# A down projection of eight units in three passes over the channels, 512 columns wide, with stores that add

## The chip, the core and the metric

The kernel runs on one NeuronCore of a Trainium2 chip. Its engines have a queue of instructions each: TensorE (PE in the profile) multiplies matrices, VectorE (DVE) and ScalarE (ACT) work on rows, GpSimd (POOL) does the same and issues some transfers, and SyncE (SP) issues most of them. Engines wait for each other and for transfers by semaphores. The metric is the device time of one execution in microseconds (us).

## What is computed

One layer of a decoder trunk on 2048 rows of 1024 channels: a mixer (sliding-window attention and a gated recurrence), then a gated MLP with a short causal convolution, then a norm. The part that matters here is the end:

```python
h = rms_norm(x, ffn_norm_g[l]) * (1 + scale_f) + shift_f
u, v = jnp.split(h @ w_up[l], 2, axis=-1)                # w_up: 1024 x 2 * 2816
u = causal_depthwise_conv(u, conv_w[l], conv_b[l])
x = x + gate_f * ((jax.nn.silu(u) * v) @ w_down[l])      # w_down: 2816 x 1024
...
return rms_norm(x, final_norm_g)
```

All of it is float32. x as it stands before the MLP is called x1; it lies in DRAM as 16 tiles of 128 rows, `x1_d` (the trace calls them x_d).

## The kernel before

**Products.** Both projections of the MLP multiply 2 x 2 blocks with seven products instead of eight (Strassen's scheme in Winograd's form), and each float32 product is made of three matmuls: both operands are split into a high part that the matmul takes exactly and the low rest, and `mm3` issues high x high, high x low, low x high. An operand is therefore seven blocks (four of the matrix, and sums of them), once as h and once as l: `Th`, `Tl` for the activations, `Sh`, `Sl` for the weights. ACT writes the h part, DVE (in places POOL) subtracts to get the l part.

**Up stage.** For each of 22 blocks of 128 channels and each half of the rows (`up`, banks `ps_u`) PE makes seven products of 512 columns; DVE and ACT make the convolution, silu and the gate into `cc`. Two blocks make a pair, j = 0 to 10; `combine_a` on POOL forms the sums of the pair's blocks (`sm` and in place) and POOL's queue stores the seven blocks to `act_d` in DRAM. `combine_w` prepares the weights' sums (`wc_d`) during the second half.

**Down stage.** It goes by `DSTEPS`: 2 halves of the 1024 output columns (dh), 8 units of 256 rows (tp), 11 pairs (j). A step has 7 products x 3 = 21 matmuls of 128x256 into seven banks (`ps_d`), which sum over the 11 pairs. For each half the S operands of all 11 pairs are resident. `build_s` loads a pair's raw blocks (`Sr`, from w_down and from `wc_d`) and splits them; half 0's are built at its first eight steps, half 1's at the steps that the table `SWITCH` gives, from the fifth pair of half 0's last unit on into the first unit of half 1. The tiles of S lie where tiles of the up stage lay, so a pair's build waits for the last reader of that memory; `S_PLACE` sets which. The activations of a step are loaded (`da`, four buffers) and split (`Th`, `Tl`, three buffers each) by `ahead`, some steps before they are used.

**A unit's end** (`d_unit` behind its loop). ACT and DVE sum the seven banks into `o` (256 rows of 512 columns), DVE multiplies by the gate (`dgate`) and adds x1's columns (`dx`), ACT squares. Half 0 stores the result times `dfin` (the norm's gain) to `xf_d`; half 1 loads that back (`df`), forms the root from both halves' squares, scales, and stores both halves to the output.

**What sets the order.** A scheduler orders each engine's instructions; `pin(True, SY)` keeps SP's in the order of the program, for the first eight steps of the stage and a few more loads.

Of the kernel before, what the change touches and what calls it, by code (L numbers as in the profile page):

```python
# [18 lines left out]
P = 128  # L19
# [34 lines left out]
def kernel(ctx, tc, x, c, ada_w, ada_b, mix_norm_g, w_in, b_in, attn_sinks, attn_out_g,  # L54
# [26 lines left out]
    wc_d = [[dram.tile([P, 4, 256], F32, name=f"wc_d{i}_{j}") for j in range(NJ)] for i in range(2)]  # L81
    xf_d = [dram.tile([P, 2, 512], F32, name=f"xf_d{i}") for i in range(NB // 2)]
# [1223 lines left out]
    for hf_ in range(T // HT):  # L1306
        for ff in range(NFF):
            cur = ups
            if ff + 1 < NFF:
                ups = prep_up(hf_, ff + 1)  # L1310
            elif hf_ == 0:
                ups = prep_up(1, 0)
            combine_acts(hf_, ff - 1)
            up(hf_, ff, cur, orders.get((hf_, ff), order))
            if hf_ == 0 and ff == 0:
                turn_block(*pend)
            if hf_ == 0 and ff in (4, 8, 12, 16):
                combine_t(ff // 4 - 1)
            if hf_ == 1 and ff < NFF - 2:
                for i in range(2 if ff > 17 else 1):  # L1320
                    combine_w(*divmod(ff if ff < 18 else 2 * ff + i - 18, NJ))
        combine_acts(hf_, NFF - 1)
# [7 lines left out]
    dr = ctx.enter_context(tc.tile_pool(name="dr", bufs=1, reuse_waits="tile"))  # L1330
    do = ctx.enter_context(tc.tile_pool(name="do", bufs=1, reuse_waits="tile"))


    S_LATE = ("8h", "8l", "9h", "9l", "10h", "10l")
    S_PLACE = ("2h", "0h", "3h", "0l", "T", "1h", "1l", "2l", "3l", "4l", "5l", "6l", "7l", "6h", "7h", "4h", "5h")

    def place(key):
        return ctx.enter_context(tc.tile_pool(name=f"ds{key}", bufs=1, reuse_waits="tile"))
    places = {key: place(key) for key in S_LATE}
    places["u"] = place("u")  # L1340
    for key in S_PLACE:
        places[key] = place(key)
    dt_ = places["T"]
    dss = ctx.enter_context(tc.tile_pool(name="dss", bufs=1, reuse_waits="tile"))

    sops = {}

    def s_op(j, hl, name, dt):
        return places[f"{j}{hl}"].tile([P, 7, 256], dt, tag=f"S{j}{hl}", name=name)

    def load_s(dh, j):

        nm = f"{dh}_{j}"
        c0 = dh * 512
        if j + 2 < NJ:
            r = s_op(j + 2, "h", f"Sr{nm}", F32)
            SY.dma_start(out=r[:, 0, :], in_=wdn_v[2 * j * P:(2 * j + 1) * P, c0:c0 + 256])
            SY.dma_start(out=r[:, 1:3, :], in_=wdn_v[(2 * j + 1) * P:(2 * j + 2) * P, c0:c0 + 512]
                         .rearrange("p (c n) -> p c n", c=2))
            SY.dma_start(out=r[:, 3:7, :], in_=wc_d[dh][j])  # L1360
            return [(slice(0, 7), r)]
        parts = []
        for i, src in enumerate((wdn_v[2 * j * P:(2 * j + 1) * P, c0:c0 + 256],
                                 wdn_v[(2 * j + 1) * P:(2 * j + 2) * P, c0:c0 + 512],
                                 wc_d[dh][j][:, 0:2, :], wc_d[dh][j][:, 2:4, :])):
            n = 1 if i == 0 else 2
            r = dr.tile([P, 2, 256], F32, tag="raw", bufs=4, name=f"dw{nm}_{i}")[:, 0:n, :]
            SY.dma_start(out=r, in_=src.rearrange("p (c n) -> p c n", c=n) if i < 2 else src)
            parts.append((slice(max(2 * i - 1, 0), 2 * i + 1), r))
        return parts  # L1370

    def build_s(dh, j):
        parts = load_s(dh, j)
        hi, lo = (s_op(j, hl, f"S{dh}_{j}{hl}", F32R) for hl in "hl")
        for sl, r in parts:
            n = sl.stop - (2 if dh == 0 and NJ - 2 > j >= 4 else 2 if dh and j + 2 < NJ else 0)
            S.activation(hi[:, sl, :], r, AF.Copy)
            V.tensor_tensor(out=lo[:, sl.start:n, :], in0=r[:, 0:n - sl.start, :], in1=hi[:, sl.start:n, :].bitcast(F32),
                            op=ALU.subtract)
            if n < sl.stop:  # L1380
                G.tensor_tensor(out=lo[:, n:, :], in0=r[:, n:, :], in1=hi[:, n:, :].bitcast(F32), op=ALU.subtract)
        sops[dh, j] = hi, lo

    raws, tts, seen = {}, {}, set()
    DSTEPS = [(dh, tp, j) for dh in range(2) for tp in range(NB // 2) for j in range(NJ)]

    def load_a(step):
        dh, tp, j = step
        nm = f"{dh}_{tp}_{j}"
        r = dr.tile([P, 7, P], F32, tag="raw", bufs=4, name=f"da{nm}")  # L1390
# [14 lines left out]
    ssall = const.tile([P, NB // 2, 2], F32, name="ssall")  # L1405

    def d_bank(name):
        turn[0] += 1
        return bank(name, ring8[turn[0] % 8])[:, 0:256]
# [10 lines left out]
    def d_unit(dh, tp):  # L1420
        nm = f"{dh}_{tp}"
        ps = {p: d_bank(f"ps_d{nm}_{p}") for p in DORDER}
        o = do.tile([P, 2, 512], F32, tag="o", name=f"o{nm}")
        u = places["u"].tile([P, 256], F32, tag="u", bufs=2, name=f"u{nm}")
        c11, c12, c21, c22 = o[:, 0, 0:256], o[:, 0, 256:], o[:, 1, 0:256], o[:, 1, 256:]

        def add(dst, p, other):
            V.tensor_tensor(out=dst, in0=ps[p], in1=other, op=ALU.add)

        sums = {1: lambda: S.activation(u, ps[1], AF.Copy), 2: lambda: add(c11, 2, u), 6: lambda: add(u, 6, u),  # L1430
                7: lambda: add(c21, 7, u), 5: lambda: (add(c22, 5, c21), add(u, 5, u)), 4: lambda: add(c21, 4, c21),
                3: lambda: add(c12, 3, u)}
        for j in range(NJ):
            ahead((dh, tp, j), 3 - (j == NJ - 1))
            th, tl = tts.pop((dh, tp, j))
            sh, sl = sops[dh, j]
            for p in DORDER:
                a, b = DPROD[p]
                mm3(ps[p], th[:, a, :], tl[:, a, :], sh[:, b, :], sl[:, b, :], j == 0, j == NJ - 1)
                if j == NJ - 1:  # L1440
# [85 lines left out]
```

## Time and profile before

| | |
|---|---|
| median of 3 runs | 2494.3 us (2492.16 to 2494.49) |
| profiled execution | 2490.66 us, its span 2488.9 us |
| PE busy | 2323.8 us, 93% of the span |
| DVE busy | 1911.0 us, 77% |
| ACT busy | 1055.6 us, 42% |
| POOL busy | 919.4 us, 37% |
| DMA | 389.90 MB, 157 GB/s over the span |
| last up matmul, last down matmul | 1972.0 and 2475.7 us from the span's start |

The span runs from the first to the last event of the profiled execution; its own time is a little longer. Shares are means over stages that differ, so what the down stage is limited by is read from that stretch of time. Matmuls' ends are modelled; the distance of their starts is the measure of their pace.

### The profile page before, as it was taken

To read this page: it belongs to the slowest core of one execution; us is meant where nothing else is said; L and a number is where in the kernel's file an instruction comes from. 1 tells how busy PE (TensorE), PEld (TensorE's weight loads), DVE (VectorE), ACT (ScalarE), POOL (GpSimd) and SP (SyncE) were. 2 spreads that over 40 slices of the span, in tenths; PEclk is the share of its full clock that TensorE was granted. 3 is DMA by queue.
4 is the path that set the end of the run, shared out by engine and by line. 5 is a ranking of instruction groups with operands and counts; after the bars stand their busy time and mean duration, and the time that the engine had idled before them with its cause. 6 is when DMAs were issued, how large, how long until landed. Compare 5 with 4: busy or idle time off the path is not lost.

```text
span 2488.9 us, 35680 instructions
## 1 busy us (share of the span) xinstructions
PE 2323.8 (93%) x13369; PEld 2010.0 (81%) x13369; DVE 1911.0 (77%) x2743; ACT 1055.6 (42%) x1776; POOL 919.4 (37%) x743
## 2 busy tenths in 40 slices
PE   5889898998989899999999999999999789997997
PEld 4778786887878688887888887788888679997997
DVE  8888778888876876568888888788877776676665
ACT  3336434623733454454333334333332344455443
POOL 6222212222322221225757564788888410011000
PEclk8999999999999999999999999999999889998999
DMA  7343233323322247664444245455454577687776
GB/s 213 90 119 98 81 91 96 94 69 101 95 68 85 85 159 246 204 204 131 139 129 144 93 140 189 158 159 163 161 157 166 199 260 218 211 283 263 260 243 203
DMA packets 337304, 389.90 MB, mean 157 GB/s; under 512 B 14069, under 2 KB 258763, under 8 KB 337131
## 3 DMA queue, kind: packets, MB, share of 16 engines
q1 hardware_dynamic: 326571, 347.25, 44.8%
q0 software_dynamic: 10560, 40.37, 4.4%
q8 instruction: 105, 1.72, 0.3%
q14 instruction: 68, 0.56, 0.1%
HBM read 293.71 MB, written 93.86 MB: 156 GB/s over the span
## 4 chain that ended last, share of the span: by engine, by line
PE 66%; DVE 13%; DMA 7%; POOL 6%; issue 5%; ACT 2%; SPq 0%; DVEq 0%; ACTq 0%; POOLq 0%
PE ps_u L46 24%; PE ps_d L46 15%; PE ps_o L46 5%; PE lv L46 3%; PE ps_hg L46 3%; PE ps_hq L46 2%; PE ps_hf L46 2%; PE ps_i L46 2%; PE att_o L46 2%; DVE ada L46 2%; DMA ada<-in_ada_w_dram 1%; POOL s L46 1%; PE ps_q L46 1%; DVE raw L46 1%; POOL sm L46 1%
## 5 line engine op out<-in xcount | busy, mean ns | idle before, releaser
L46 DVE TENSOR_TENSOR Tl<-da,Th 128x896 fp32r<-128x896 f32 x176 | 201.5, 1154 | 119.9 <-ACT Th L46 119.8
L46 ACT ACTIVATE Th<-da 128x896 fp32r<-128x896 f32 x176 | 166.5, 949 | 194.6 <-PE ps_d L46 161.5
L46 DVE SCALAR_TENSOR_TENSOR cc<-ub,cols,cc 128x1024 f32<-128x1024 f32 x88 | 153.4, 1743 | 14.3 <-ACT cc L46 12.0
L46 PE MATMUL lv<-a_q,K 128*128 128x128 f32 (+2 forms) x768 | 78.6, 262 | 43.8 <-DVE K L46 39.7
L46 PEld LDWEIGHTS lv<-a_q,K 128*128 128x128 f32 (+2 forms) x768 | 70.4, 173 | 56.5 <-DVE K L46 28.2
L46 DVE TENSOR_TENSOR cc<-cc,v 128x1024 f32<-128x1024 f32 x44 | 64.9, 1476 | 44.5 <-ACT cc L46 44.5
L46 POOL TENSOR_TENSOR s<-wu_0r,s 128x512 f32<-128x512 f32 x44 | 59.3, 1347 | 107.4 <-DVE ws_0l L46 14.8
L46 ACT ACTIVATE cc<-cc 128x1024 f32<-128x1024 f32 x44 | 46.7, 1060 | 122.5 <-DVE cc L46 122.5
L46 POOL TENSOR_TENSOR s<-wu_1r 128x512 f32<-128x512 f32 x44 | 68.8, 1563 | 70.1 <-DVE t_T4l L46 15.8
L46 POOL TENSOR_TENSOR wu_1r<-wu_0r,wu_1r 128x512 f32<-128x512 f32 x44 | 92.9, 2111 | 3.1
L46 POOL MEMSET AT<- 128x512 f32 x16 | 8.5, 532 | 230.3 <-PE ho L46 208.3
L46 POOL TENSOR_TENSOR pl<-raw,ph 128x512 fp32r<-128x512 f32 x32 | 44.6, 1395 | 101.2 <-ACT ph L46 101.2
L46 POOL TENSOR_SCALAR rv_d<-ssd 128x2 f32<-128x2 f32 x8 | 1.5, 192 | 208.5 <-DVE ssd L46 208.5
L46 POOL TENSOR_TENSOR S_0l<-Sr,S_0h 128x512 fp32r<-128x512 f32 x1 | 2.6, 2601 | 201.9 <-ACT S_0h L46 201.9
L46 POOL TENSOR_TENSOR s<-s,wu_0r 128x512 f32<-128x512 f32 x44 | 73.7, 1674 | 0.0
L46 DVE TENSOR_TENSOR v<-ps_u,v 128x512 f32<-128x512 f32 x88 | 60.4, 686 | 15.5 <-PE ps_u L46 12.2
L46 DVE COPY_PREDICATED AT<-lev,lv 128x512 f32<-128x512 uint32 (+1 forms) x96 | 70.0, 729 | 2.4 <-PE lv L46 1.1
L46 DVE TENSOR_TENSOR ada<-ada,cond 128x1024 f32<-128x1024 f32 (+1 forms) x37 | 54.9, 1483 | 15.3 <-DMA ada<-in_ada_w_dram 13.9
L46 ACT ACTIVATE cc<-ub,cols 128x1024 f32<-128x1024 f32 x44 | 54.5, 1240 | 24.7 <-DVE ub L46 24.7
L46 DVE TENSOR_TENSOR a_q<-a_q,tot 128x256 f32<-128x256 f32 x96 | 52.8, 550 | 9.5 <-PE lv L46 8.5
L46 DVE TENSOR_TENSOR ub<-ps_u,u 128x512 f32<-128x512 f32 x88 | 60.0, 682 | 0.1
L46 DVE TENSOR_TENSOR ot<-ps_o,gate 128x512 f32<-128x512 f32 x32 | 22.0, 688 | 46.6 <-PE ps_o L46 45.6
(2138 smaller groups left out, 9178.8 us busy)
## 6 DMA issues: line engine op xcount, KB each, us to landing
da<-act_d SPq DMA_DIRECT2D x176, 448.0 KB, 4.0
wu_0r<-in_w_up_dram SPq DMA_DIRECT2D x44, 512.0 KB, 4.5
wu_1r<-in_w_up_dram SPq DMA_DIRECT2D x44, 512.0 KB
act_d<-cc POOLq DMA_DIRECT2D x44, 512.0 KB, 4.0
ada<-in_ada_w_dram SPq DMA_DIRECT2D x40, 512.0 KB, 6.4
act_d<-sm POOLq DMA_DIRECT2D x22, 768.0 KB, 4.2
x<-in_x_dram SPq DMA_DIRECT2D x26, 512.0 KB, 5.8
Sr<-wc_d SPq DMA_DIRECT2D x18, 512.0 KB, 7.1
```

The lines of the kernel that those rows point to most:

```text
L46: ins = fn(*args, **kwargs)
```

## The change

The stage's order is turned over. Instead of two halves of the columns with all 11 pairs resident, there are three passes over the pairs (0 to 2, 3 to 5, 6 to 10), each over all 8 units and all 1024 columns: `DSTEPS` has 88 steps of 21 matmuls of 128x512. A pass sums only over its own pairs. At a unit's end passes 0 and 1 multiply by the gate and hand both tiles of 128 rows to POOL's queue, whose transfer adds them to `x1_d` (`accum_op=ALU.add`); pass 2 loads the so summed `x1_d`, adds its own part, and makes the norm and the output. `xf_d`, `dx` of half 0 and `df` go.

Five places for a pair's S operands take turns (pair j uses place j modulo 5). The first three pairs are loaded raw into places that are free until later (`load_first`) and split in four parts; every later pair is brought in two half loads through two buffers (`half_rows`, which are also used for x1 in pass 2), each split in place of use when `bring` says. SP is in the order of the program for the whole stage. `combine_w` forms the same weight sums from other loads. The last pair's activations of the second half of rows are stored raw (`raw_d`) by POOL's queue, and `last_pair` loads, combines and stores them behind step (0, 1, 0).

The diff, cut to its core:

```diff
-    wc_d = [[dram.tile([P, 4, 256], F32, name=f"wc_d{i}_{j}") for j in range(NJ)] for i in range(2)]
-    xf_d = [dram.tile([P, 2, 512], F32, name=f"xf_d{i}") for i in range(NB // 2)]
+    wc_d = [dram.tile([P, 4, 512], F32, name=f"wc_d{j}") for j in range(NJ)]
+    raw_d = dram.tile([P, 2, HT], F32, name="raw_d")
...
-        combine_acts(hf_, NFF - 1)
+        if hf_ == 0:
+            combine_acts(hf_, NFF - 1)
+        else:
+            for i in range(2):
+                G.dma_start(out=raw_d[:, i, :], in_=acts[i])
...
+    PASSES = (range(0, 3), range(3, 6), range(6, NJ))
+    NS = 5
...
+    def half_rows(name):
+        return places["part"].tile([P, D], F32, tag="sp", bufs=2, name=name)
+    S_PARTS = (slice(0, 1), slice(1, 3), slice(3, 5), slice(5, 7))
...
+    def new_s(j):
+        sops[j] = [s_op(f"{j % NS}{hl}", f"S{j}{hl}", F32R) for hl in "hl"]
+    def load_first(j):
+        r = s_op(("3h", "3l", "4h")[j], f"Sr{j}", F32)
+        for i, sl in enumerate(S_PARTS):
+            load_part(j, i, r[:, sl, :])
+            chunks[j, i] = r[:, sl, :]
+    def load_chunks(j, ii):
+        for i in ii:
+            sl = S_PARTS[i]
+            n = sl.stop - sl.start
+            chunks[j, i] = half_rows(f"Sp{j}_{i}").rearrange("p (a n) -> p a n", a=2)[:, 0:n, :]
+            load_part(j, i, chunks[j, i])
+    def split_chunks(j, ii):
+        if j not in sops:
+            new_s(j)
+        hi, lo = sops[j]
+        for i in ii:
+            sl = S_PARTS[i]
+            split(chunks.pop((j, i)), hi[:, sl, :], lo[:, sl, :], lo_eng=V)
...
-    DSTEPS = [(dh, tp, j) for dh in range(2) for tp in range(NB // 2) for j in range(NJ)]
+    DSTEPS = [(pi, tp, j) for pi in range(3) for tp in range(NB // 2) for j in PASSES[pi]]
...
-        return bank(name, ring8[turn[0] % 8])[:, 0:256]
+        return bank(name, ring8[turn[0] % 8])
...
+        if pi < 2:
+            for i in (1, 0):
+                V.tensor_tensor(out=o[i], in0=o[i], in1=dgate, op=ALU.mult)
+                G.dma_start(out=x1_d[2 * tp + i], in_=o[i], accum_op=ALU.add)
             return
...
+        for i in (1, 0):
+            V.tensor_tensor(out=o[i], in0=o[i], in1=dgate, op=ALU.mult)
+            V.tensor_tensor(out=o[i], in0=o[i], in1=prev[i], op=ALU.add)
+            S.activation(prev[i], o[i], AF.Square, accum_out=ss[:, i:i + 1])
+        r = rstd_of(places["ss"], ss, 2, D, f"d{tp}")
+        for i in (1, 0):
+            V.scalar_tensor_tensor(out=o[i], in0=o[i], scalar=r[:, i:i + 1], in1=dfin, op0=ALU.mult, op1=ALU.mult)
+            parts.append((out_v[(2 * tp + i) * P:(2 * tp + i + 1) * P, :], o[i]))
...
+    behind(0, 1, 0, last_pair)
+    def bring(j, steps):
+        behind(*steps[0], load_chunks, j, (0, 1))
+        behind(*steps[1], split_chunks, j, (0, 1))
+        behind(*steps[1], load_chunks, j, (2, 3))
+        behind(*steps[2], split_chunks, j, (2, 3))
+    bring(3, ((0, 3, 0), (0, 3, 1), (0, 3, 2)))
+    bring(4, ((0, 5, 0), (0, 5, 1), (0, 5, 2)))
+    bring(5, ((0, 6, 2), (0, 7, 0), (0, 7, 1)))
+    bring(6, ((1, 2, 3), (1, 2, 4), (1, 2, 5)))
+    bring(7, ((1, 4, 3), (1, 4, 4), (1, 4, 5)))
+    bring(8, ((1, 6, 5), (1, 7, 3), (1, 7, 4)))
+    bring(9, ((1, 7, 4), (1, 7, 5), (2, 0, 6)))
+    bring(10, ((2, 0, 6), (2, 0, 7), (2, 0, 8)))
```

Three places show how the engines' rows move. The first is ACT's queue at the start of the down stage (cc_21 is the last gated block, its second row there is silu; S0h is pair 0's high part, Th that of step 0). Before:

```order
L46 ACTIVATE cc_21_16833<-ub_21_16730,cols 128x1024
L46 ACTIVATE cc_21_16833<-cc_21_16833 128x1024
L46 ACTIVATE S_0h<-Sr_0_16936 128x1792
L46 ACTIVATE Th_0_0_16946<-da_0_0_16944 128x896
L46 ACTIVATE S_1h<-Sr_1_16950 128x1792
L46 ACTIVATE Th_0_1_16960<-da_0_1_16958 128x896
```

and now:

```order
L46 ACTIVATE cc_21_16837<-ub_21_16734,cols 128x1024
L46 ACTIVATE S0h<-Sr_16906 128x512
L46 ACTIVATE S0h<-Sr_16906 128x1024
L46 ACTIVATE cc_21_16837<-cc_21_16837 128x1024
L46 ACTIVATE S0h<-Sr_16906 128x1024 x2
L46 ACTIVATE Th_0_16937<-da_0_16911 128x896
L46 ACTIVATE S1h<-Sr_16913 128x512
L46 ACTIVATE S1h<-Sr_16913 128x1024 x3
L46 ACTIVATE Th_1_16951<-da_1_16918 128x896
```

S0h is now made in four pieces, two of them ahead of silu, and Th stands behind the fourth. The second place is PE's first step of the stage (ps_d_0_1 is product 1's bank of unit 0). Before:

```order
L46 MATMUL ps_d_0_1_16988<-S_0h,Th_0_0_16946 128x256
L46 MATMUL ps_d_0_2_16989<-S_0h,Th_0_0_16946 128x256
L46 MATMUL ps_d_0_6_16990<-S_0h,Th_0_0_16946 128x256
L46 MATMUL ps_d_0_7_16991<-S_0h,Th_0_0_16946 128x256
L46 MATMUL ps_d_0_5_16992<-S_0h,Th_0_0_16946 128x256
L46 MATMUL ps_d_0_1_16988<-S_0l,Th_0_0_16946 128x256
```

and now:

```order
L46 MATMUL ps_d_0_1_16969<-S0h,Th_0_16937 128x512
L46 MATMUL ps_d_0_1_16969<-S0l,Th_0_16937 128x512
L46 MATMUL ps_d_0_1_16969<-S0h,Tl_0_16938 128x512
L46 MATMUL ps_d_0_2_16970<-S0h,Th_0_16937 128x512
L46 MATMUL ps_d_0_2_16970<-S0l,Th_0_16937 128x512
L46 MATMUL ps_d_0_2_16970<-S0h,Tl_0_16938 128x512
```

Before, five products had their high matmuls ahead of the first that needs a low part; now the second and the third matmul need S0l and Tl. The third place is SP's queue at the last change of weights (Sr and Sp are raw weights, da raw activations, wc_d_119 to wc_d_121 the sums of pairs 8 to 10). Before, in the first unit of half 1:

```order
L46 DMA da_0_4_19711<-act_d_4_93 128x896
L46 DMA Sr_5_19734<-in_w_down_dram 128x256
L46 DMA Sr_5_19734<-in_w_down_dram 128x512
L46 DMA Sr_5_19734<-wc_d_5_127 128x1024
L46 DMA da_0_5_19747<-act_d_5_94 128x896
L46 DMA xf_d_140<-o_7_19337 128x1024
L46 DMA da_0_6_19774<-act_d_6_95 128x896
```

and now, from the last unit of pass 1 into the first of pass 2:

```order
L46 DMA Sp_2_18664<-wc_d_119 128x1024
L46 DMA Sp_3_18666<-wc_d_119 128x1024
L46 DMA da_8_18672<-act_d_8_97 128x896
L46 DMA Sp_0_18699<-in_w_down_dram 128x512
L46 DMA Sp_1_18701<-in_w_down_dram 128x1024
L46 DMA da_9_18739<-act_d_9_98 128x896
L46 DMA Sp_2_18747<-wc_d_120 128x1024
L46 DMA Sp_3_18749<-wc_d_120 128x1024
L46 DMA da_10_18766<-act_d_10_99 128x896
L46 DMA Sp_0_18793<-in_w_down_dram 128x512
L46 DMA Sp_1_18795<-in_w_down_dram 128x1024
L46 DMA da_6_18801<-act_d_6_95 128x896
```

A pair was three loads into a tile of its own; now it is four, two at a time, each into one of the two buffers behind the loads that used it last.

## Rows read from the trace of the kernel before

**Rows 1.** The page's slices: busy tenths of PE in 40 equal slices.
```profile
PE   5889898998989899999999999999999789997997
```

**Rows 2.** Windows, down stage, ps_d alone: us, busy us (count) per engine, clock, DMA.
```profile
1972.00:2060.00 88.00, 66.87 (x458) 63.28 (x459) 2.68 (x7) 0.75 (x2) 0.86 0.83 284
2060.00:2200.00 140.00, 140.00 (x1159) 139.06 (x1158) 13.61 (x36) 1.83 (x5) 1.00 0.72 220
2200.00:2300.00 100.00, 86.24 (x644) 82.86 (x643) 7.94 (x21) 0.75 (x2) 0.93 0.80 276
2300.00:2475.70 175.70, 175.00 (x1441) 173.14 (x1439) 17.47 (x46) 2.58 (x7) 1.00 0.76 247
```

**Rows 3.** The same view over 100 us of the up stage, ps_u alone.
```profile
1840.00:1940.00 100.00, 100.00 (x439) 82.01 (x438) 22.84 (x34) 2.59 (x5) 1.00 0.49 158
```

**Rows 4.** Timeline of PE, down stage's start: start, duration, operation, idle before, releaser.
```profile
1971.62 0.39 PE L46 MATMUL ps_u<-t_T4h,wvs_21l 128*128 128x512 f32 x1
1977.50 1.43 PE L46 MATMUL ps_d<-S_0h,Th 128*128 128x256 f32 x5 [5.49 <-ACT Th L46]
...
1985.87 1.68 PE L46 MATMUL ps_d<-S_1l,Th 128*128 128x256 f32 x7
1987.36 1.03 PE L46 MATMUL ps_d<-S_1h,Tl 128*128 128x256 f32 x7
...
1996.75 1.86 PE L46 MATMUL ps_d<-S_2l,Th 128*128 128x256 f32 x7 [7.53 <-DVE S_2l L46]
```

**Rows 5.** Timeline of ACT, same stretch.
```profile
1973.96 1.06 ACT L46 ACTIVATE cc<-cc 128x1024 f32<-128x1024 f32 x1 [5.41 <-DVE cc L46]
...
1976.51 0.93 ACT L46 ACTIVATE Th<-da 128x896 fp32r<-128x896 f32 x1
```

**Rows 6.** Timeline of DVE, same stretch.
```profile
1976.64 2.87 DVE L46 TENSOR_TENSOR S_0l<-Sr,S_0h 128x1792 fp32r<-128x1792 f32 x1 [0.36 <-DMA Sr<-in_w_down_dram]
...
1994.67 2.03 DVE L46 TENSOR_TENSOR S_2l<-Sr,S_2h 128x1792 fp32r<-128x1792 f32 x1 [7.96 <-issue]
```

**Rows 7.** Tile act_d, 1960 to 2000 us: who waited for it, landing.
```profile
  DVE S_2l L46: 8.0, 1
...
DMA to landing us min/median/max: 7.8/8.3/8.9
```

**Rows 8.** Groups of DVE's instructions by form, whole span.
```profile
L46 DVE TENSOR_TENSOR Tl<-da,Th 128x896 fp32r<-128x896 f32 x176 | 201.5, 1154 | 119.9 <-ACT Th L46 119.8
...
L46 DVE TENSOR_TENSOR v<-ps_u,v 128x512 f32<-128x512 f32 x88 | 60.4, 686 | 15.5 <-PE ps_u L46 12.2
...
L46 DVE TENSOR_TENSOR o<-o,dgate 128x1024 f32<-128x1024 f32 x16 | 19.5, 1218 | 0.0
```

**Rows 9.** Timeline of PE after a wait, up stage; six rows between.
```profile
1956.99 0.79 PE L46 MATMUL ps_u<-t_T2h,ws_21l 128*128 128x512 f32 x1 [3.33 <-DVE ws_21l L46]
...
1960.12 0.40 PE L46 MATMUL ps_u<-t_T2h,ws_21h 128*128 128x512 f32 x1
```

**Rows 10.** Window at the down stage's start, all engines.
```profile
1972.00:1980.00 8.00, 1.88 (x8) 1.58 (x8) 6.47 (x5) 6.04 (x6) 3.65 (x3) 0.82 1.02 387
```

**Rows 11.** Timeline of ACT at the second half's weights.
```profile
2252.28 1.70 ACT L46 ACTIVATE S_6h<-Sr 128x1792 fp32r<-128x1792 f32 x1 [2.88 <-DMA Sr<-wc_d]
```

**Rows 12.** DMA issues, 1960 to 2489 us: count, KB each, median to landing.
```profile
da<-act_d SPq DMA_DIRECT2D x176, 448.0 KB, 4.0
Sr<-wc_d SPq DMA_DIRECT2D x18, 512.0 KB, 7.1
...
xf_d<-o SPq DMA_DIRECT2D x8, 512.0 KB, 4.3
```

**Rows 13.** Timeline at the program's end: PE, DVE, ACT.
```profile
2475.46 0.28 PE L46 MATMUL ps_d<-S_10h,Tl 128*128 128x256 f32 x1
...
2476.63 0.41 DVE L46 TENSOR_TENSOR o<-ps_d,u 128x256 f32<-128x256 f32 x1
...
2484.20 1.33 ACT L46 ACTIVATE df<-df,rr_d 128x512 f32<-128x512 f32 x2 [3.27 <-DMA df<-xf_d]
```

More of the change, by code (lines that the diff above doesn't have):

```diff
@@ L1339 @@
[L1339 to L1382, printed above, removed]
+        return ctx.enter_context(tc.tile_pool(name=f"d_{key}", bufs=1, reuse_waits="tile"))
@@ new lines, with s_op @@
+    places = {key: place(key) for key in ("raw", "u", "o", "2l", "2h", "1l", "1h", "3h", "0h", "0l", "T", "4l", "gate",
+                                          "part", "3l", "4h", "fin", "ss")}
+    sops, chunks = {}, {}
+    def s_op(key, name, dt):
+        return places[key].tile([P, 7, 512], dt, tag=f"S{key}", name=name)
+    def half_rows(name):
+        return places["part"].tile([P, D], F32, tag="sp", bufs=2, name=name)
+    S_PARTS = (slice(0, 1), slice(1, 3), slice(3, 5), slice(5, 7))
@@ L1422, in d_unit, with stores @@
+    parts = []
+    def stores():
+        while parts:
+            dst, src = parts.pop(0)
+            SY.dma_start(out=dst, in_=src)
+    def d_unit(pi, tp):
+        js = PASSES[pi]
+        nm = f"{pi}_{tp}"
         ps = {p: d_bank(f"ps_d{nm}_{p}") for p in DORDER}
-        o = do.tile([P, 2, 512], F32, tag="o", name=f"o{nm}")
-        u = places["u"].tile([P, 256], F32, tag="u", bufs=2, name=f"u{nm}")
-        c11, c12, c21, c22 = o[:, 0, 0:256], o[:, 0, 256:], o[:, 1, 0:256], o[:, 1, 256:]
+        prev = o = u = None
@@ L1427, in add @@
         def add(dst, p, other):
             V.tensor_tensor(out=dst, in0=ps[p], in1=other, op=ALU.add)
[L1430 to L1436, printed above, removed]
+        for j in js:
+            ahead((pi, tp, j), 3 - (j == js[-1]))
+            if j == js[1]:
+                stores()
+            if j == js[-2] and pi == 2:
+                prev = [half_rows(f"dx{tp}_{i}") for i in range(2)]
+                for i in range(2):
+                    SY.dma_start(out=prev[i], in_=x1_d[2 * tp + i])
+            th, tl = tts.pop((pi, tp, j))
+            sh, sl = sops[j]
+            if j == js[-1]:
+                o = [places["o"].tile([P, D], F32, tag="o", bufs=3, name=f"o{nm}_{i}") for i in range(2)]
+                u = places["u"].tile([P, 512], F32, tag="u", name=f"u{nm}")
+                c11, c12, c21, c22 = o[0][:, 0:512], o[0][:, 512:], o[1][:, 0:512], o[1][:, 512:]
+                sums = {1: lambda: S.activation(u, ps[1], AF.Copy), 2: lambda: add(c11, 2, u), 6: lambda: add(u, 6, u),
+                        7: lambda: add(c21, 7, u), 5: lambda: (add(c22, 5, c21), add(u, 5, u)),
+                        4: lambda: add(c21, 4, c21), 3: lambda: add(c12, 3, u)}
@@ L1500 @@
+    stores()
+    pin(False, SY)
 _INS = ['x', 'c', 'ada_w', 'ada_b', 'mix_norm_g', 'w_in', 'b_in', 'attn_sinks', 'attn_out_g', 'hgrn_lb_logits',
```

144 lines of the change are left out of this document (63 added, 81 removed).

## The prediction, made before the changed kernel had run

> **What bounds the kernel now.** The slices of the profile's page come first [rows 1]: in the last fifth of the span, the last nine slices of 62 us, PE is busy 9 tenths or more in five; 7 and 8 where the stage begins, 7 in the slice from 2240 us, 7 at the end. PE is the bound there, with holes. The windows over the stage size them [rows 2]. Between 2060 and 2200 us nothing holds PE: 1159 matmuls of 256 columns in 140.00 us, 0.1208 us each, at a granted clock of 1.00. The stage issues 2 halves x 8 units x 11 pairs x 21 = 3696 of them, 446.5 us at that pace, and lasts from the last up matmul (1972.0) to the last down matmul (2475.7), 503.7 us. So 57.2 us are lost, nearly all in two windows: 88.00 us with 458 matmuls (55.3 us of work), 32.7 lost at the stage's start; 100.00 us with 644 (77.8), 22.2 lost where the second half's weights come; and 1.6 in the last window. The window of the up stage, where matmuls are 512 wide, gives 439 in 100 us at clock 1.00, 0.2278 us each [rows 3].
>
> The sum is made against the profiled run's 2490.7 us (span 2488.9 and 1.8 around it); the median of the runs shown, 2494.3, lies 3.6 above it, and those 3.6 are put back at the end.
>
> **Pace: -25.5.** The change issues (3 + 3 + 5) x 8 x 21 = 1848 matmuls of 512 columns for the same work. At 0.2278 us that is 421.0 instead of 446.5. The two paces differ by 0.2278 - 2 x 0.1208 = -0.0138 us for equal columns, so a matmul costs here about 14 ns beyond its columns at either width, and half the matmuls save that half. A rule speaks against this: the Trainium skill, "TensorE: Matmul & The Clock Gate", section Back-to-back issue gap, gives a warm matmul its columns at 2.4 GHz plus some 2.5 ns. An estimate by that page is 109 ns and 216 ns for the two widths, and a gain of 4.7 us only; the trace does not agree with its size, and the row's pace is what the sum uses.
>
> **Start: -21.7.** Now PE waits twice [rows 4]: 5.49 us for ACT's first Th, and 7.53 us for DVE's S_2l, and from 1977.50 it runs at half pace to 1987.36 at least (seven matmuls of 256 in 1.49 us from the row at 1985.87 to that one). Ahead of the first Th ACT does the gated activation's silu at 1973.96 and then S_0h [rows 5]; both stay in the changed order, with two small parts of S0h ahead of silu. From silu's 1973.96, 1.0 for it, two parts of 1.0 and Th's 0.93 put the first matmul at 1977.9, 0.4 later than now. The wait for S_2l goes: DVE's S_2l began 7.96 us late [rows 6], and it is the one that waited 8.0 us for the stores of POOL's combined acts, which took 8.3 us to land [rows 7]: the memory of S_2l had been that of the combined tile. The change takes that combination out of the path: the last pair is stored raw and combined later. What is late next is the third matmul (S0h with Tl), because products are now finished one by one: DVE has behind the last gating 0.69 + 3 x 1.22 for S0l in its four parts (durations by [rows 8]: 686 ns for 512 columns, 1218 ns for 1024), then Tl 1.15, and a multiplication of the gate: Tl_0 is there at about 1980.6. Pairs 1 and 2 follow at 0.69 + 3 x 1.22 + 1.15 = 5.5 us each, so Tl_2 at 1991.6, and its step of 4.8 us ends at 1996 to 1998. Without any wait three steps of 21 x 0.2278 would end at 1986.4 from 1972.0. The loss is 10 to 12; I take 11 instead of 32.7.
> The clock costs part of this. After a wait of 3.33 us in the up stage seven matmuls took 3.13 us, 0.45 each, until the next at 1960.12 ran at 0.23 [rows 9]; that is 1.6 us lost. At the start of the down stage half pace held for 9.9 us, which would lose some 4. These are its two ends, and they lie inside the 11, because DVE's chain and not PE sets the times of steps 1 and 2.
> The three pairs' loads are 4.6 MB with acts. DMA moved 387 GB/s at a share of 1.02 [rows 10], so 11.9 us from about 1969, and S2h is wanted at 1982: in time by a little. A load that lands at twice that costs up to 8.
>
> **Switch: -18.2.** Before, the second half's 11 pairs are loaded and split within some 16 steps of 2.5 us, and ACT waits for them (2.88 us for one pair's products at 2252.28 [rows 11]). After, pairs 3 to 5 come one at a time in pass 0, a unit and more ahead of their use: nothing is exposed at the change from pass 0 to 1. From pass 1 to 2 it is tight. Pair 8 takes the place of pair 3, so its split can start only after step (1,7,3); then pair 9's and 10's halves follow through two buffers of two half pairs, each freed by the split before. Counted from the end of (1,7,3), with a landing of 4 us and 3 us for two splits and the issue, five such stages of some 7 us end at 34. Step (2,0,10) would start 28.6 after it (two steps of pass 1, four of pass 2, 4.8 us each), but its last quarter is wanted only by products 6 and 4; PE's order puts 7, 5, 3 and the next unit's first two in front. That leaves a wait of about 2. At 5 us it is 5, at 7.1 us, what the loads of pairs show in the DMA row [rows 12], 15. The 4.0 of a da load of 448 KB in the same group is nearest in size; the two larger prices belong to stretches of 0.8 DMA share. I take 4 for the whole switch, 2 to 15.
>
> **Other waits: +0.4.** A unit of three steps lasts 14.35 us. DVE then has three Tl (3.46), seven sums of 512 (4.8) and two gate products (2.4), 10.7; with a pair's split, 4.34 more, 15.0, which is over the unit by 0.7 in three units of pass 0 and two of pass 1; th and tl have three buffers each, which hold 4.8 us ahead. POOL's four operations of the deferred pair slow DVE while they run (S_0l took 2.87 us beside POOL and S_2l 2.03 alone [rows 6]): another 3 us, in a unit without a split. I take 2 instead of 1.6, bounds 0 and 8.
>
> **The adding stores: 0.** 32 stores of 512 KB now add to x1 in DRAM, and no row of before shows one. From below it is a plain store of the same size, 4.3 us to landing; from above a load and then a store, 7.1 + 4.3 = 11.4 [rows 12]. The o tiles have three buffers, each written by DVE again 1.5 units later at the earliest, so DVE would wait for a landing over some 9.7 us. What they hold in the DMA engines decides: a plain one is 0.524 MB at 387 GB/s, 1.36 us of all engines [rows 10]. With k times that, pass 0 has 28.4 us of da loads, 14.2 of pairs, 7.5 of the deferred pair and 21.7 k in 114.8 us: full at k = 3.0. Pass 1 is full at k = 3.3. A plain store and a load together would be k = 2, which fits; I take 0 and keep both ends. The Trainium skill, "Collectives: The Full Stack", section The bandwidth ceiling, says that an adding transfer reads two sources for one write. By that page k would be some 2 plain transfers, an estimate; no run here shows one.
> The half results' 8 stores and 8 reloads of before (512 KB each) go, and 176 loads of acts become 88: the DMA share of 0.72 to 0.83 falls, which gives PE nothing where it did not wait.
>
> **Tail: +1.6.** Now 13.2 us run from the last matmul's end at 2475.74 to the span's end: sums until 2477.05, gate and addition 2.5, squares, the wait for the first half's result (ACT starts 2484.20 behind it), stores [rows 13]. After: the last sums are 512 wide (1.4), two rows of gate, addition and square one after the other (4 x 1.22 and 1.25), 1.1 for the root, two scalings of 1.27, a store of 512 KB at 3.1 to 4.3. That is 14.8; 13.5 to 17.
>
> **Sum.** -25.5 - 21.7 - 18.2 + 0.4 + 1.6 = -63.4; 2490.7 - 63.4 = 2427.3, and 3.6 more is 2431.
>
> **Rivals.**
> Adding stores that fill the DMA engines, but not to break-even. For it: share is 0.72 to 0.83 before, and nothing shows their price. Against it: the freed loads. With k = 3.5, pass 0 is longer by 11.3 and pass 1 by 3.7, 2446; k = 4 gives +36.6, 2468; to 2480.
> The other side, slower than before: the same mechanism from k = 4.62 on. The loads of acts queue behind the adding stores in both passes, and 21.7 x (2k - 6.3) exceeds 63.4. At k = 5 it is +80, 2511. Against it: a k of 2 is what a load and a store together need.
> The switch at a landing of 7.1 us: +11, 2442. For it: the pairs' row in the DMA group [rows 12]. Against it: these landings belong to a crowded stretch.
> Wide matmuls that save little: if their pace in this stage is twice the 256's, 0.2416, the pace gives nothing, 446.5 in place of 421.0, and at a gain of 5 it is 2451. For it: a stage with more work on DVE beside it could pace PE. Against it: 439 matmuls in 100 us [rows 3]. The page on TensorE named above would have it so.
> No difference: gains in the holes are given back by the switch and the stores, 2494.
>
> **How the numbers follow.** The forecast holds 0.58, with 2412 to 2446 by the bounds of start (-3 to +8), switch (2 to 15), waits and tail. Adding stores below break-even 0.16, the slow switch 0.10, the lost pace 0.06, beyond break-even 0.08, no difference 0.02. The first four together are faster, 0.90. About 0.2% is what a measurement of this kernel can tell from none. 2410 to 2470 leaves out break-even, no difference, part of the filled DMA and some ends of the forecast, under 0.2.
>
> **What would show it.** Pace: 1848 matmuls at 0.228 where nothing waits. Start: the first at 1978, unit 0 ending at 1996 to 1998, and no DVE wait for a store of POOL. Switch: PE's waits at step (2,0,10), 2 to 5 us, and none at (1,0,3). Stores: no DVE wait on an o tile, DMA share under 0.8 in passes 0 and 1. Tail: 14 to 16 us. A DMA share near 1.0 in pass 0 with PE waiting for Th would prove the forecast wrong, and by the size of k how far.

## The result, and the profile after

The changed kernel takes 2465.4 us (median of 4, 2456.9 to 2467.7) against 2493.3: a ratio of 0.988 (95% interval 0.9866 to 0.9895), 28 us faster. The forecast was 63 us faster, 2431; the time lies inside its range, and more than half of the gain that it promised is missing.

The profiled execution took 2456.9 us (span 2455.1), the fastest of the four. Its down stage lasts 464.0 us from the start of the last up matmul to that of the last down matmul; before it was 503.8. The runs further down come from other batches; the kernel before ran in each of them too, with medians of 2494.4 to 2495.4 us, so their times can be set beside these to some 2 us. Where nothing holds PE, the windows show the pace of the 512-wide matmuls, and it is even a little better than that of the up stage [rows 3] (columns as there):

```profile
2300.00:2400.00 100.00, 100.00 (x443) 82.84 (x442) 18.20 (x28) 2.40 (x4) 1.00 0.49 180
```

A unit of 63 matmuls takes 14.28 us from its first start to the next unit's, 0.2267 each. The starts of units are therefore a ruler for every loss. This table is worked out from them (a unit's length in the PE timeline less 14.28, or 23.80 in pass 2; units not named lose nothing):

```
              last up  first down  losses by unit (pass, tp)                                 whole
              matmul   matmul      (0,0) (0,3) (0,5) (1,0) (1,2) (1,4) (2,0)                 stage
after         1975.95  1982.13      4.3   6.5   5.4   2.3   5.0   5.5  10.2                  464.0
forecast                           start 11 in all    2 for all of these   4                 438
```

The start came as forecast: PE begins 6 us after the last up matmul and the third matmul waits for Tl (timeline of PE; before [rows 4]):

```profile
1975.95 0.39 PE L46 MATMUL ps_u<-t_T4h,wvs_21l 128*128 128x512 f32 x1
1982.13 0.79 PE L46 MATMUL ps_d<-S0h,Th 128*128 128x512 f32 x1 [5.80 <-ACT Th L46]
1984.46 0.79 PE L46 MATMUL ps_d<-S0h,Tl 128*128 128x512 f32 x1 [1.10 <-DVE Tl L46]
```

So did the tail: 14.8 us from the last matmul's end to the span's end (timeline of PE, DVE, SP; before [rows 13]).

```profile
2439.96 0.39 PE L46 MATMUL ps_d<-S10h,Tl 128*128 128x512 f32 x1
...
2448.75 2.48 DVE L46 SCALAR_TENSOR_TENSOR o<-o,rr_d,dfin 128x1024 f32<-128x1024 f32 x2 [2.31 <-POOL rr_d L46]
...
2450.06 1.53 SPq L46 DMA_DIRECT2D out_dram<-o  x2
```

What was not forecast are five units that lose 24.7 us together, each beside a `bring`. In unit (0,3) the PE timeline shows three waits for banks that the sums of unit (0,2) had not yet read, and behind the third matmuls at half pace (0.43 us from one start to the next; the granted clock from 2037.68 to 2040.41 is 0.50, the level of 1.2 GHz):

```profile
2033.20 0.50 PE L46 MATMUL ps_d<-S0h,Th 128*128 128x512 f32 x1 [1.75 <-DVE u L46]
...
2035.48 0.50 PE L46 MATMUL ps_d<-S0h,Th 128*128 128x512 f32 x1 [1.32 <-DVE o L46]
...
2037.68 0.80 PE L46 MATMUL ps_d<-S0h,Th 128*128 128x512 f32 x1 [1.23 <-DVE u L46]
2038.27 0.63 PE L46 MATMUL ps_d<-S0l,Th 128*128 128x512 f32 x1
2038.70 0.63 PE L46 MATMUL ps_d<-S0h,Tl 128*128 128x512 f32 x1
```

Of the 24.7 us, 14.7 are PE's waits themselves; most of the rest is half pace behind them. The prediction counted a wait without what follows it, except at the start.

DVE's timeline says why PE waits. Between the first and the second sum of unit (0,2) stands the split of pair 3, which is not needed before pass 1, and DVE stands still for 4.71 us in front of it:

```profile
2026.46 0.68 DVE L46 TENSOR_TENSOR o<-ps_d,u 128x512 f32<-128x512 f32 x1
2031.85 0.69 DVE L46 TENSOR_TENSOR S3l<-Sp,S3h 128x512 fp32r<-128x512 f32 x1 [4.71 <-ACT S3h L46]
2032.46 0.68 DVE L46 TENSOR_TENSOR u<-ps_d,u 128x512 f32<-128x512 f32 x1
2033.60 1.22 DVE L46 TENSOR_TENSOR S3l<-Sp,S3h 128x1024 fp32r<-128x1024 f32 x1 [0.46 <-ACT S3h L46]
2034.75 0.68 DVE L46 TENSOR_TENSOR o<-ps_d,u 128x512 f32<-128x512 f32 x1
```

ACT waits in its turn for the load, which SP had issued 8.2 us earlier, behind two adding stores of POOL (timelines of ACT, SP and POOL):

```profile
2031.19 0.63 ACT L46 ACTIVATE S3h<-Sp 128x512 fp32r<-128x512 f32 x1 [5.22 <-DMA Sp<-in_w_down_dram]
...
2022.96 1.25 SPq L46 DMA_DIRECT2D Sp<-in_w_down_dram  x2
...
2019.28 0.86 POOL L46 DMA_DIRECT2D x_d<-o  x1 [5.05 <-DVE o L46]
2020.42 0.83 POOL L46 DMA_DIRECT2D x_d<-o  x1 [0.28 <-DVE o L46]
```

While the adding stores run, the windows of all engines show the DMA engines full at half the rate of a full stretch before (387 GB/s at share 1.02 [rows 10]); the last two columns are DMA share and GB/s:

```profile
2020.00:2022.00 2.00, 2.00 (x11) 1.65 (x10) 1.65 (x3) 0.95 (x1) 0.98 (x2) 1.00 1.03 236
2022.00:2024.00 2.00, 2.00 (x10) 1.69 (x9) 0.56 (x1) 0.00 (x0) 0.00 (x0) 1.00 1.03 190
2024.00:2026.00 2.00, 2.00 (x10) 1.65 (x9) 0.55 (x1) 1.51 (x2) 0.00 (x0) 1.00 1.00 207
...
2028.00:2030.00 2.00, 2.00 (x11) 1.65 (x10) 0.00 (x0) 0.00 (x0) 0.00 (x0) 1.00 1.02 400
```

At the change to pass 2 PE waits twice for bank sums and then for the last pair, in four places such as this (timeline of PE); its waits add up to 5.3 us of the 10.2 lost:

```profile
2262.22 0.49 PE L46 MATMUL ps_d<-S10h,Th 128*128 128x512 f32 x1 [0.87 <-ACT S10h L46]
```

Two theories were set against each other. By the first, the order is the cause: the scheduler put the splits among the sums on DVE and ACT. By the second, the adding stores are: they fill the DMA engines and the pairs' loads land late. A third was that DVE simply has too much to do in such a unit (15.0 us by the prediction's sum).

### The profile page after: what moved, and what is told of

It reads as the page before. It is cut to its first block, busy times and chain, and to the rows that moved or that the text cites. A ratio compares the mean times of both kernels' runs of the same rounds, so it can differ in the third digit from the quotient of the medians.

```text
span 2455.1 us, 31438 instructions
## 1 busy us (share of the span) xinstructions
PE 2296.7 (94%) x11521; PEld 1908.9 (78%) x11521; DVE 1903.9 (78%) x2737; ACT 971.7 (40%) x1658; POOL 917.9 (37%) x760
## 3 DMA queue, kind: packets, MB, share of 16 engines
HBM read 250.19 MB, written 107.49 MB: 146 GB/s over the span
## 4 chain that ended last, share of the span: by engine, by line
PE 66%; DVE 13%; DMA 8%; issue 7%; POOL 3%; ACT 2%; SPq 0%; DVEq 0%; POOLq 0%; ACTq 0%
PE ps_u L46 28%; PE ps_d L46 10%; PE ps_o L46 6%; PE lv L46 3%; PE ps_hg L46 3%; PE ps_hq L46 2%; PE ps_hf L46 2%; PE ps_i L46 2%; PE att_o L46 2%; DVE ada L46 2%; DMA Sp<-in_w_down_dram 2%; DMA ada<-in_ada_w_dram 2%; PE ps_q L46 1%; DVE AT L46 1%; DVE raw L46 1%
## 5 line engine op out<-in xcount | busy, mean ns | idle before, releaser
L46 ACT ACTIVATE Th<-da 128x896 fp32r<-128x896 f32 x88 | 83.9, 953 | 230.7 <-PE ps_d L46 210.7
L46 DVE TENSOR_TENSOR Tl<-da,Th 128x896 fp32r<-128x896 f32 x88 | 97.1, 1111 | 73.0 <-ACT Th L46 72.7
L46 POOL DMA_DIRECT2D x_d<-o x32 | 27.2, 858 | 237.0 <-DVE o L46 237.0
L46 POOL TENSOR_TENSOR s<-wu_0r,s 128x512 f32<-128x512 f32 x44 | 59.2, 1345 | 107.3 <-DVE ws_0l L46 14.7
L46 DVE TENSOR_TENSOR o<-ps_d,u 128x512 f32<-128x512 f32 x72 | 49.2, 684 | 15.4 <-ACT u L46 13.9
```

What stands on the lines that cost most here:

```text
L46: ins = fn(*args, **kwargs)
```

## The experiments

**The changed kernel again (e0_again).** No edit.

> The changed kernel once more, unedited. Its four runs so far went from 2456.9 to 2467.7 us, and the profiled one was the fastest. If the spread belongs to single executions and not to the chip, the median lies again at 2460 to 2468. The losses per unit in the trace should repeat: 24 us in the five units (0,3), (0,5), (1,0), (1,2), (1,4) and 10 in (2,0).

2466.6 us (2461.3 to 2470.6). The losses repeat: 27.8 us in the five units, 10.6 in (2,0), stage 467.6. The five losses alone thus differ by 3.1 us between two executions of one kernel. This trace's span is 11.2 us longer than the first one's, and 7.6 of that lies ahead of the down stage: its last up matmul starts at 1983.55 instead of 1975.95.

```profile
1983.55 0.39 PE L46 MATMUL ps_u<-t_T4h,wvs_21l 128*128 128x512 f32 x1
```

**Plain stores (e1_plain_store).**

```diff
-                G.dma_start(out=x1_d[2 * tp + i], in_=o[i], accum_op=ALU.add)
+                G.dma_start(out=x1_d[2 * tp + i], in_=o[i])
```

> The 32 transfers store without adding (the addition to x1 and to the other passes' sums is left out; every order and every wait stays). Theory of the order: DVE's split of a brought pair stands among the sums of a unit and waits for a load that is issued too late anyway; without the addition the five losses of 24 us stay, 2455 to 2467. Theory of the adding stores: an adding store of 512 KB keeps all DMA engines for about 3 us where a plain one takes 1.4, so the pairs' loads that are issued behind two of them land late; without the addition the first half load lands in 5 us instead of 8, each of the five losses falls from 5 to under 2, 2438 to 2450.

2439.6 us (2438.0 to 2445.6), 26 less than the changed kernel. Each engine's instructions stand in the order of the changed kernel. The five losses fall from 24.7 to 8.1, that of (2,0) from 10.2 to 6.2. The price of adding is in the DMA view from 2000 to 2240 us of either kernel, first the changed one (30 adding stores), then this (32 plain ones); the POOL queue's line ends with its share of 16 engines, the issue's line with us to landing:

```profile
q0 software_dynamic: 4320, 15.73, 38.6%
...
x_d<-o POOLq DMA_DIRECT2D x30, 512.0 KB, 6.5
```
```profile
q0 software_dynamic: 4330, 15.77, 18.7%
...
x_d<-o POOLq DMA_DIRECT2D x32, 512.0 KB, 4.0
```

An adding store holds all engines for 0.386 x 240 / 30 = 3.09 us, a plain one for 1.40: k = 2.2. Pair 3's first quarter is there after 5.7 us instead of 8.2 (issued 2025.85), and one wait of the three is left in (0,3):

```profile
2031.56 0.63 ACT L46 ACTIVATE S3h<-Sp 128x512 fp32r<-128x512 f32 x1 [1.95 <-DMA Sp<-in_w_down_dram]
...
2038.01 0.50 PE L46 MATMUL ps_d<-S0h,Th 128*128 128x512 f32 x1 [1.24 <-DVE u L46]
```

The theory of the adding stores holds here. What is left, 0.7 to 1.9 in each unit, goes when the splits leave their place among the sums as well (e8_order_plain).

**The order kept (e2_dve_order).**

```diff
         for tp in range(NB // 2):
+            pin(pi < 2 and (pi, tp) > (0, 0), V, S)
             for j in d_unit(pi, tp):
```

> DVE and ACT keep the order of the program from the second unit of pass 0 to the end of pass 1, so that a pair's split stands behind the sums of the unit before and not among them; loads and adding stores are as they were. Theory of the order: the banks come free in time, the five losses (24 us) go but for some 3, 2436 to 2445. Theory of the adding stores: the late loads then hold the splits, which hold the Th and Tl behind them, and PE waits for these instead; at least half of the 24 us stays, 2450 to 2465. If DVE's work in such a unit (15.0 us by the prediction's sum) is the bound, 0.7 us in each of five units stays, 2440.

2443.2 us (2441.2 to 2446.2), 23 less, with every adding store in place. Pair 3's first half load is issued 6.1 us ahead of unit (0,3), behind the same two adding stores, as before (6.3). Four of the five units lose nothing. In (0,3) the sums now run through, and the split stands behind them, with no wait in front of it (timeline of DVE):

```profile
2036.13 0.68 DVE L46 TENSOR_TENSOR o<-ps_d,u 128x512 f32<-128x512 f32 x1
...
2042.00 1.82 DVE L46 TENSOR_TENSOR S3l<-Sp,S3h 128x512 fp32r<-128x512 f32 x2
```

(1,0) loses 5.8: there the order of the program itself has pair 5's second split in front of unit (0,7)'s sums, and ACT's copy of the first bank stands behind it (timeline of PE).

```profile
2110.80 0.50 PE L46 MATMUL ps_d<-S3h,Th 128*128 128x512 f32 x1 [3.47 <-ACT u L46]
```

The theory of the order holds, the one of DVE's load falls: the units with splits run at 14.28.

**Loads a step earlier (e3_early_load).**

```diff
-    bring(3, ((0, 3, 0), (0, 3, 1), (0, 3, 2)))
+    bring(3, ((0, 2, 2), (0, 3, 1), (0, 3, 2)))
```

and so for pairs 4 to 7.

> The first half loads of pairs 3 to 7 are issued one step (4.8 us) earlier; the adding stores stay, and the splits still stand among the sums for the larger part. Theory of the order together with late data: the data is there when the split's turn comes, most of the 24 us goes, 2440 to 2450. Theory that the order alone does it, whatever the data: the splits' own 1.9 us stay in front of the sums, a loss of some 2 in each of the five units, 2450 to 2455. Theory of the adding stores alone: the loads move ahead of them, so the same 2440 to 2450.

2462.8 us (2459.7 to 2466.9): all three expectations missed, the five units still lose 24.7. The loads were asked for a step earlier, but SP, in order behind four loads of activations, issued pair 3's at 2026.42, 1.4 earlier counted from the unit's start, and ACT had its data 8.5 us later. And the scheduler moved the split forward with the load, now in front of the Tl and of the first sum (timelines of SP and DVE):

```profile
2026.42 1.73 SPq L46 DMA_DIRECT2D Sp<-in_w_down_dram  x2
...
2035.64 0.69 DVE L46 TENSOR_TENSOR S3l<-Sp,S3h 128x512 fp32r<-128x512 f32 x1 [8.51 <-ACT S3h L46]
2036.48 1.09 DVE L46 TENSOR_TENSOR Tl<-da,Th 128x896 fp32r<-128x896 f32 x1
2037.49 0.68 DVE L46 TENSOR_TENSOR o<-ps_d,u 128x512 f32<-128x512 f32 x1
```

**Pair 5 behind the sums too (e4_order_late5).**

```diff
-    bring(5, ((0, 6, 2), (0, 7, 0), (0, 7, 1)))
+    bring(5, ((0, 6, 2), (0, 7, 0), (1, 0, 3)))
```

> The kernel with DVE and ACT in the order of the program, and the second split of pair 5 moved from inside the last unit of pass 0 to behind the first step of pass 1. With the order alone PE still lost 5.7 us at the first unit of pass 1, waiting for ACT's copy of a bank, which stood behind that split. If the place in the queue is the cause, this loss goes and nothing else changes: 2436 to 2440. If the load's lateness is, the split blocks the Th behind it instead, and it stays at 2442 to 2446.

2440.9 us (2438.6 to 2442.6), ratio to before 0.978 (0.9765 to 0.9796). The time lies between the two expectations; the trace decides for the first: all five losses are gone, (2,0) loses 11.0, and the stage lasts 440.7. Against e2_dve_order the stage of the traced execution is 6.8 us shorter and its up stage ends 3.3 later; the medians are 2.3 apart, within the spread of either.

**A longer chain (e5_switch_fine).** Three `half_rows` buffers instead of two, three raw ones instead of four, and the quarters of pairs 8 to 10 loaded one stage earlier.

> As e4_order_late5, and the chain of loads at the last change of pass is lengthened: three load buffers instead of two, and quarters of a pair loaded one stage earlier; the raw activations have three buffers instead of four to make room. If the chain of load and split through two buffers is what costs 10 to 12 us at the first unit of pass 2, half of it goes: 5 to 6 us less than e4_order_late5, 2431 to 2435. If the place in the queues is what costs there (ACT's copy of a bank behind a split of pair 8 or 9), nothing changes: 2436 to 2440. If three buffers for raw activations are too few, PE waits for Th all over the stage, above 2445.

2441.8 us (2440.9 to 2442.8), as e4_order_late5, and (2,0) loses 12.8. The first expectation missed. Three quarters of pair 8 now wait in their buffers, but the fourth is issued at 2215.18, right behind two adding stores (2212.71 and 2213.84), and ACT has it 8.9 us later (timeline of ACT):

```profile
2224.04 1.06 ACT L46 ACTIVATE S8h<-Sp 128x1024 fp32r<-128x1024 f32 x1 [7.14 <-DMA Sp<-wc_d]
```

Pair 10's second quarter goes the same way: it is issued at 2238.28 behind the next two stores, and ACT has it 9.2 us later.

**256 columns (e6_narrow).** Each matmul as two of half the columns.

```diff
-                mm3(ps[p], th[:, a, :], tl[:, a, :], sh[:, b, :], sl[:, b, :], j == js[0], j == js[-1])
+                for n in (slice(0, 256), slice(256, 512)):
+                    mm3(ps[p][:, n], th[:, a, :], tl[:, a, :], sh[:, b, n], sl[:, b, n], j == js[0] and n.start == 0,
+                        j == js[-1] and n.start == 256)
```

> Every matmul of the stage as two of 256 columns, 3696 in all, everything else as in the changed kernel. By the rows of before (0.1208 us each) and of after (1848 at 0.2267) the work alone grows by 446.5 - 418.9 = 27.6 us; with the waits that hide a part, 2485 to 2496. By the rule of the Trainium skill, TensorE: Matmul & The Clock Gate, section Back-to-back issue gap, it would grow by 4.7, 2468 to 2474.

2478.6 us (2474.2 to 2480.3). A unit without waits takes 15.12 instead of 14.28, 0.1200 for each matmul:

```profile
2330.00:2430.00 100.00, 100.00 (x835) 100.00 (x834) 18.20 (x28) 2.32 (x4) 1.00 0.49 174
```

So a matmul costs 0.84 us / 63 = 13 ns beyond its columns, as the prediction read it from [rows 2, 3]; the 2.5 ns of the Trainium skill's section that the expectation names are not seen. The 17 units without waits grow by 18.2 in all (10 by 0.84, 7 by 1.40) and the stage by 18.0: in the seven with waits the longer work is hidden. That takes 9.6 us off the 27.6, and so the expectation is missed. The medians are 13 apart, the stages 18.0, or 14.4 against the trace of e0_again.

**The pair combined at once (e7_pair_at_once).** `combine_acts` again for the last pair, and no `last_pair`.

> The last pair's activations are combined at once by POOL again, as before the change; nothing is deferred. If the deferral is what took DVE's wait of 8 us for the combined acts' stores out of the start, PE loses 6 to 9 us more in the first unit, 2471 to 2476. If the new places of the weights alone did it, only DVE's slower work beside POOL costs, 2 to 3 us in the first unit, and the deferred pair's transfers go from pass 0: 2463 to 2469.

2481.0 us (2477.2 to 2483.1), 15 more. Unit (0,0) loses 14.5 instead of 4.3, by one wait of PE for DVE's Tl, which starts at 2000.95; ACT waits up to the same moment for the last store of the combined pair (timelines of PE and ACT):

```profile
2002.10 0.79 PE L46 MATMUL ps_d<-S0h,Tl 128*128 128x512 f32 x1 [11.27 <-DVE Tl L46]
...
2000.99 0.95 ACT L46 ACTIVATE Th<-da 128x896 fp32r<-128x896 f32 x1 [8.59 <-DMA act_d<-sm]
```

So the deferral takes 10.8 us off the start, 0.5 of it ahead of the first down matmul; that is more than expected. The five units lose 6.2 more than in the first trace of the changed kernel and 3.1 more than in e0_again; no run says why.

**Order and plain stores (e8_order_plain).** The edits of e1_plain_store and e4_order_late5.

> As e4_order_late5 with plain stores in place of the adding ones (the addition to x1 and to the other passes' sums is left out). What is left of the loss is then the start and the switch alone. If the adding stores cost only through the two places in pass 1 where they delay the last pairs' loads, the first unit of pass 2 loses 5 to 6 us instead of 11, and nothing else changes: 2434 to 2437. If the chain through two buffers is the cause of all of it, 11 stay: 2440 to 2443.

2435.9 us (2429.1 to 2438.0). (2,0) loses 5.0 instead of 11.0, and the other units behind the start lose 0.4 at most. ACT's wait for pair 8's second half load, first in e4_order_late5, then here:

```profile
2225.80 2.12 ACT L46 ACTIVATE S8h<-Sp 128x1024 fp32r<-128x1024 f32 x2 [8.75 <-DMA Sp<-wc_d]
```
```profile
2213.74 1.06 ACT L46 ACTIVATE S8h<-Sp 128x1024 fp32r<-128x1024 f32 x1 [4.20 <-DMA Sp<-wc_d]
```

**Passes of 4, 3 and 4 pairs (e9_434).**

```diff
-    PASSES = (range(0, 3), range(3, 6), range(6, NJ))
+    PASSES = (range(0, 4), range(4, 7), range(7, NJ))
```

with pair 3 brought in unit (0,0), the other `bring` calls moved to match, and DVE and ACT in order.

> Passes of 4, 3 and 4 pairs in place of 3, 3 and 5, order of the program kept on DVE and ACT as in e2_dve_order, adding stores as they are. At each change of pass only two pairs must come into places that were in use until then (one and three before). If the chain of loads at the change to pass 2 costs more than in proportion to its length, the losses of 11 fall to 2 to 3 at each of the two changes, and the fourth pair costs 1 to 2 at the start: 2434 to 2439. If the two chains cost as much together as the one, 2440 to 2445. If the fourth pair is late in the first unit (its split stands behind three others on DVE), above 2445.

2441.0 us (2437.3 to 2446.1), as e4_order_late5. The fourth pair costs next to nothing at the start (unit (0,0) loses 4.8, in e4_order_late5 4.4), but (1,0) loses 7.9 and (2,0) 6.6: in the trace two short chains cost 14.5 us together and the one long 11.0.

**The same with the splits behind the sums (e10_434_behind).** Pair 6's first split, pair 9's second and pair 10's go behind the unit's sums.

> As e9_434, with the splits that stood on ACT and DVE between the last steps of a pass and that unit's sums moved behind the sums (pair 6 to behind the unit, the second half of pair 9 too, pair 10 one step later). In e9_434 PE waited 4.3 and 3.4 us at the two changes of pass for ACT's copy of a bank, with 7.9 and 6.5 us lost in all. If the place in the queue is the cause, 1 to 2 are left at each, 2429 to 2433. If the late loads are, the splits that come later make the new pair late instead and PE waits for S6h or S10h: 2438 to 2444, as e9_434.

2444.6 us (2441.4 to 2445.3). The waits for ACT's copy are gone, and the new pairs are late in their place (timeline of PE), 7.6 and 7.4 lost:

```profile
2161.97 0.80 PE L46 MATMUL ps_d<-S6h,Th 128*128 128x512 f32 x1 [3.79 <-ACT S6h L46]
...
2289.32 1.22 PE L46 MATMUL ps_d<-S10h,Th 128*128 128x512 f32 x2 [5.33 <-ACT S10h L46]
```

Moving the splits wins nothing at the changes of pass, and the place in the queue decides which wait shows the loss. This run alone does not prove the landing times to be the cause: with two buffers a later split also frees its buffer later, and the next loads are issued later (pair 6's last two at 2152.53 and 2153.67, behind its first split). That plain stores take 6.0 of the 11.0 away (e8_order_plain) shows the part of the adding stores.

**The kernel before again (before_again).** No edit, one execution, 2497.4 us.

> The kernel before, unedited, for a second trace. In the traces of the changed kernel and its variants the last up matmul starts between 1976 and 1986 us, in the one trace of before at 1971.6. If that is the spread of single executions, it is later here too, 1973 to 1980, and the down stage lasts the same 503.7 us; if the change itself makes the earlier stages later, it stays at 1971 to 1973.

Its last up matmul starts at 1977.31 and its stage lasts 504.8: the earlier stages differ by 5.7 us between two executions of one kernel, 5.0 of it ahead of the first up matmul (1107.4 and 1112.3 us).

```profile
1977.31 0.39 PE L46 MATMUL ps_u<-t_T4h,wvs_21l 128*128 128x512 f32 x1
```

## Why the prediction was wrong, by its own steps

- **Pace, -25.5: right.** 1848 x 0.2267 = 418.9 us against 421.0 forecast; e6_narrow measures the price of a matmul by itself.
- **Start, -21.7: right in size.** The wait and unit (0,0) lose 10.2 together against 11, and the third matmul comes 8.1 us behind the last up matmul's end (forecast 8.6). Of the 22.5 us gained, e7_pair_at_once gives 10.8 to the deferral; the other 11.7 belong to the rest of the new start (places, order, weights in parts), which no run takes apart. Its 4.6 MB are two pairs' loads with acts, not three, which are 6.9; it did no harm, since pair 0's loads went out at 1956 and only pairs 1 and 2 came behind.
- **Other waits, +0.4: the step that failed.** 24.7 us are lost in five units where 2 were forecast for all. The step added up DVE's operations in a unit, found 15.0 us against 14.35, and let three buffers of Th and Tl absorb it. It took the queue for a sum of work and did not look at its order: the sums that free PE's banks stand behind splits that nobody needs for a long time, and the splits wait for a load. e4_order_late5 takes all five losses away with the adding stores in place, e2_dve_order four of them.
- **Adding stores, 0: the size was right, the reading of it wrong.** k is 2.2 where a plain store and a load together (2) were taken as fitting. The Trainium skill, "Collectives: The Full Stack", section The bandwidth ceiling, says that an add needs two source reads for one write. The time in the DMA engines is near that; the second read itself is not seen, for the profile's page counts the same 250.19 MB read from HBM with adding and with plain stores. The step compared k with a whole pass (full at 3.0), but two such stores come at once: 6.2 us of full DMA engines per unit, and a load issued into that is there after 8 us. e1_plain_store takes 16.6 of the 24.7 away. Order and stores each take the larger part away alone, so their shares can't be added: a load has to be late and something has to stand behind it.
- **Switch, -18.2: too small a loss, 10.2 against 4.** It lies inside the bound of 15, though that bound was loosely worked out: by its own five stages a landing of 5 us would give 7 and one of 7.1 us 17.5, where it wrote 5 and 15. In the trace of the changed kernel the chain's quick loads are there after 2.6 to 4.2 us, those beside adding stores after 5.7 to 7.9. Plain stores take 4.1 (e1_plain_store) or 6.0 (e8_order_plain) of the loss away, and 5.0 stay, near the 4. A buffer more (e5_switch_fine) and shorter chains (e9_434, e10_434_behind) change nothing; in each of them some load of the chain still falls behind two adding stores.
- **Tail, +1.6: right.** 14.8 us as forecast.
- **Bounds of the forecast itself.** Those of its steps add up to 2423 to 2458, where it wrote 2412 to 2446. The measured 2465 lies outside both; only the share of the rivals takes the whole range to 2470.
- **Outside the sum.** In the profiled execution the up stage ends 4.3 us later than in the trace of before. With that the terms close: 2427.3 - 2.1 - 0.8 + 22.7 + 6.2 + 0.0 + 4.3 = 2457.6, and 2456.9 was measured. The median is 8.5 above that execution, and by the two traces of it most of such a difference lies ahead of the down stage.

The sum had nothing for the up stage, and the traces say what the 4.3 us are. Up to the first up matmul every engine has the same instructions in the same order in both kernels; it starts at 1107.4 and 1112.3 us in the two traces of before, at 1110.2 to 1117.4 in the twelve of the changed kernel and its variants. In the first pair of traces 2.8 of the 4.3 us come from there; the kernel before differs by 5.0 from itself, so nothing lays that to the change. Most of the up stage takes 1.1 us less. Its last 308 matmuls take longer: 75.8 and 76.4 us before, 77.3 to 79.3 in all twelve others, 2.6 us more in the first pair. There PE waits for a split of block 20's weights, as in this row, and in most of them for block 21's `ub`, and runs at half pace behind; before waits for neither:

```profile
1933.57 0.50 PE L46 MATMUL ps_u<-t_T3h,wvs_20l 128*128 128x512 f32 x1 [0.53 <-DVE wvs_20l L46]
```

So the change makes the up stage's end 1.0 to 3.5 us longer, a small cost that the forecast had at nothing; what delays the split was not sought.

Of the rivals, the adding stores that fill the DMA engines come nearest, in another form than was written: not a pass filled on the mean (the DMA share is 0.82 in pass 0 and 0.76 in pass 1), but a stretch behind each unit.

## What to carry to other kernels

A wait is found in a queue's order and not in an engine's sum of work: where a scheduler orders the instructions, look at what stands behind each one that waits for a load, and keep what frees a bank in front of it. An adding store of 512 KB is cheap on the mean and dear where it falls: give the loads that are issued behind it the landing time of full DMA engines, here 8 to 9 us where a quiet one took about 4. Count with a wait of PE what half pace behind it costs, here about two thirds of the wait once more. Asking for a load earlier did nothing in e3_early_load, because the queue that issues it was hardly free earlier and the instruction that uses it moved forward too.

## What the runs showed of the hardware

An adding store into DRAM holds the DMA engines 2.2 times as long as a plain one (3.09 against 1.40 us of all 16 for 512 KB), and its landing takes 6.5 us instead of 4.0. A matmul with its own weights costs 13 ns beyond its columns at 256 and at 512 (2 x 0.1200 - 0.2267 us). Half pace behind a wait has no fixed length: behind a wait of 3.1 to 3.3 us in the up stage for the same split (ws_21l) it lasted 3.1 us in both traces of before [rows 9], 5.2 in that of the changed kernel (1960.35 to 1965.56), and in the other eleven anything from almost none (0.3) to 6.1.
